# The last four channel tiles of a ConvFFN down projection, moved from plain products to seven block products

## The chip, the cores and the metric

One NeuronCore of a Trainium2 chip runs the whole block for one sequence of 1024 tokens in float32. The metric is device time in microseconds (us) of one execution, and lower is better. Five engines take part: PE (TensorE, matmuls and their weight loads), DVE (VectorE), ACT (ScalarE), POOL (GpSimd) and SP (SyncE, which here only issues transfers). Each runs its own list of instructions in order and waits for the others where it needs their results.

## The reference, cut to what matters

```python
h = rmsnorm(x, norm_mix_g)                      # x: (1, 1024, 1024)
z = h @ w_in                                    # -> A_h, A_B, A_C, B_val, B_gate
yA = A_B * dwconv3(A_C * A_h)
yB = silu(layernorm(dwconv31(B_val * sigmoid(B_gate)) + b))
x = x + concat(yA, yB) @ w_out
h = rmsnorm(x, norm_ffn_g)
g = dwconv3(h @ w_gate)                         # 2816 channels
v = h @ w_up
x = x + (silu(g) * v) @ w_down                  # 2816 -> 1024
return rmsnorm(x, norm_final_g)
```

The change lies in the product with `w_down` and in the final norm, which needs, for every token, the sum of squares over all 1024 outputs.

## The kernel before, in words

Tokens lie along the free axis, in two halves of 512 (`h` = 0 and 1). Channels lie on the 128 partitions: 8 tiles of the model dimension (`d` = 0 to 7) and 22 tiles of the FFN dimension (`f` = 0 to 21). Every float32 operand of a matmul is split into a high and a low part (`split`: ACT copies the high part, DVE subtracts it, L131 and L93), and one product of 128x128 by 128x512 is three matmuls: high by high, high by low, low by high.

**Seven block products.** A product of a 2x2 arrangement of blocks is done with seven block products in place of eight. For the down projection the two rows are two output tiles of a pair `dp` (`m` = 0, 1), the two columns are the token halves, and the inner two are an even and an odd FFN tile. The class `Pair` holds the seven methods. They add into three PSUM banks `a`, `b` and `c`, and after some of them DVE (or ACT and POOL) adds a bank into the residual tile `xf[2*dp+m]`, half `h`:

- `m1` (A11 B11 into `a`) and `m2` (A12 B21 into `b`) both go to (m, h) = (0, 0),
- `m6` (S2 T2 added to `a`) goes to (0, 1), `m7` (S3 T3 added to `a`) to (1, 1), `m4` (A22 T4 added to `a`) to (1, 0),
- `m5` (S1 T1 into `c`) goes to (1, 1), `m3` (S4 B22 added to `c`) to (0, 1).

So the first half of the pair's two tiles is complete with m1, m2, m6, m7 and m4. S1 to S4 are sums of weight blocks, made on POOL (`Sums`, L511) and split on ACT and DVE. T1 to T4 are differences of FFN activations, made on POOL in `ff_done` (L90) when an odd tile `f` is finished; B11, B21, B22 and the T blocks go to DRAM buffers `yd*`, each by a store of 256 KB that SP issues, and come back later through `load_op`, which loads a block and splits it.

**Rounds.** FFN tiles 0 to 17 are worked in NCH = 3 rounds (`ch`) of PPC = 3 pairs of tiles. In a round the four pairs of output tiles come as two couples (`couples`), and the products of a couple stand on PE as m1, then m3 of the couple before, m6, m2, m7, m5, m4. While the last couple of a round runs, `load_op` refills each operand's blocks in the arena `R` as soon as PE has read them.

**The tail.** FFN tiles 18 to 21 (NTAIL = 4) are stored whole in `ytail` and multiplied plainly: `tail_mm` does 4 x 3 matmuls (L152 to L154) for one output tile and one half into a bank `y`. All eight tiles of half 0 come first, then the eight of half 1. After each, `done` adds the bank to the residual on DVE (L1028), ACT squares it (L1030) and DVE adds the square to `accs[h]` (L1032); `scale` multiplies by the norm's weight on ACT (L1024). When half 0 is summed, one matmul with ones (`total3`, L1019) sums over partitions, ACT takes the root (L1067), DVE the reciprocal (L1069, row `rf`), and POOL multiplies the eight tiles of half 0 (`fin`, L1037), which SP stores. For half 1 the last tile is done in three pieces of columns (192, 192, 128): add (L1080), square on DVE (L1081), sum on PE (L1083 to L1085), root, reciprocal (L1092), then `fin` of the eight tiles, five on DVE and three on POOL, and the stores.

**What sets the order.** In blocks under `manual_schedule` the named engines keep the order of the code; the rest, and SP's issues, are ordered by the scheduler when the program is built. In the last block all four computing engines are listed in code order, but they can be filled in among instructions of the block before.

## Time and profile before

| | |
|---|---|
| time, median of 3 runs | 1000.0 us (999.8 to 1000.95) |
| the profiled execution | 1000.93 us, with a span of 999.1 us |
| PE busy | 967.5 us (97%), 4208 matmuls |
| DVE busy | 755.6 us (76%) |
| ACT busy | 452.8 us (45%) |
| POOL busy | 477.0 us (48%) |
| DMA | 112.56 MB, mean 113 GB/s |
| mean granted TensorE clock | 0.993 of full speed |

The span runs from the first to the last instruction of the profiled execution; the time of an execution is 1.8 us more. A row of a timeline gives start, duration, engine, line, operation, out<-in tiles, and in brackets how long the engine sat idle before it and what ended that. A row of the chain of waits gives start, duration and what was done on the path that ended last. Matmuls overlap: one is shown as 0.39 us, but they follow each other at about 0.23 us.

### The profile page before, as it was taken

The numbers are of one execution on the slowest core, as the hardware profiler recorded it, in microseconds if no ns is written. First come the engines' busy times: TensorE is split into PE (matmuls) and PEld (weight loads), VectorE is DVE, ScalarE is ACT, GpSimd is POOL, SyncE is SP. The second block draws the span as 40 slices with busy tenths as digits, with TensorE's granted clock in tenths as the row PEclk, the third lists the DMA queues.
The fourth block names the chain that finished last, engine by engine and source line by source line (L and its number), as shares of the span: only waits on it lengthen the run. The fifth ranks groups of instructions, "written<-read, shape, count | busy, mean of one in ns | idle before, by whom it ended". The sixth has DMA issues, their size and how long they took to land.

```text
span 999.1 us, 11602 instructions
## 1 busy us (share of the span) xinstructions
PE 967.5 (97%) x4208; PEld 790.8 (79%) x4208; DVE 755.6 (76%) x888; ACT 452.8 (45%) x632; POOL 477.0 (48%) x303
## 2 busy tenths in 40 slices
PE   7999999999999999999999999999998999999994
PEld 5788888888878887788888888888886787878883
DVE  7899999999578897855655565565569798796556
ACT  7454422234564456434444443444457263544353
POOL 4289754353853006554455456365336744352006
PEclk9999999999999999999999999999999999999998
DMA  6211111113554204143143133134284663643105
GB/s 257 85 44 63 43 45 61 42 64 106 193 190 153 76 0 158 64 148 106 64 145 108 64 124 129 64 101 141 70 287 130 220 207 96 194 127 109 61 1 169
DMA packets 63274, 112.56 MB, mean 113 GB/s; under 512 B 5488, under 2 KB 27120, under 8 KB 62960
## 3 DMA queue, kind: packets, MB, share of 16 engines
q1 hardware_dynamic: 62640, 110.65, 33.1%
q10 hardware_dynamic: 576, 1.17, 0.3%
q8 instruction: 33, 0.54, 0.2%
q14 instruction: 25, 0.20, 0.1%
HBM read 84.79 MB, written 27.00 MB: 112 GB/s over the span
## 4 chain that ended last, share of the span: by engine, by line
PE 81%; DVE 9%; ACT 3%; issue 2%; DMA 1%; POOL 1%; POOLq 0%; SPq 0%; DVEq 0%; ACTq 0%
PE a L557 30%; PE mm L166 20%; PE c L557 15%; PE b L557 7%; DVE r L93 2%; PE c L692 1%; PE a L692 1%; PE mm L153 1%; PE mm L152 1%; PE mm L154 1%; PE y L154 1%; PE y L152 1%; PE y L153 1%; DMA raw<-wgate 1%; ACT whi L131 1%
## 5 line engine op out<-in xcount | busy, mean ns | idle before, releaser
L166 PE MATMUL mm<-r,whi 128*128 128x512 f32 x576 | 155.8, 389 | 0.0
L557 PE MATMUL a<-r,whi 128*128 128x512 f32 x472 | 145.7, 390 | 0.4 <-ACT a L542 0.4
L323 DVE SCALAR_TENSOR_TENSOR cv<-u,cst,cv 128x512 f32<-128x512 f32 x203 | 138.9, 751 | 1.7 <-ACT cv L317 1.2
L511 POOL TENSOR_TENSOR s<-raw,s 128x512 f32<-128x512 f32 (+1 forms) x31 | 57.5, 1854 | 161.5 <-DVE wlo L93 161.5
L166 PEld LDWEIGHTS mm<-r,whi 128*128 128x128 f32 x576 | 108.1, 188 | 22.6
L557 PE MATMUL c<-r,whi 128*128 128x512 f32 x392 | 121.1, 390 | 0.0
L93 POOL TENSOR_TENSOR wlo<-raw,whi 128x1024 fp32r<-128x1024 f32 x30 | 77.5, 2586 | 88.0 <-ACT whi L131 88.0
L131 ACT ACTIVATE whi<-raw 128x1024 fp32r<-128x1024 f32 (+1 forms) x68 | 69.2, 1020 | 103.5 <-PE mm L166 32.0
L557 PEld LDWEIGHTS a<-r,whi 128*128 128x128 f32 x472 | 88.4, 188 | 19.7 <-ACT a L542 0.8
L511 POOL TENSOR_TENSOR s<-up 128x512 f32<-128x512 f32 (+1 forms) x31 | 42.0, 1354 | 116.7 <-DMA up<-wup 96.8
L557 PE MATMUL a<-r,wlo 128*128 128x512 f32 x236 | 92.2, 391 | 2.8 <-DVE wlo L93 2.8
L166 PE MATMUL mm<-r,wlo 128*128 128x512 f32 x288 | 90.0, 389 | 0.0
L557 PEld LDWEIGHTS c<-r,whi 128*128 128x128 f32 x392 | 73.8, 188 | 16.0
L542 ACT ACTIVATE a<-a 128x512 f32<-128x512 f32 x80 | 47.5, 595 | 66.9 <-PE a L557 64.2
L131 ACT ACTIVATE whi<-s 128x1024 fp32r<-128x1024 f32 (+1 forms) x52 | 52.5, 1010 | 53.5 <-PE c L557 39.8
L557 PE MATMUL c<-r,wlo 128*128 128x512 f32 x196 | 76.5, 390 | 0.0
L635 DVE TENSOR_TENSOR t<-a,c 128x512 f32<-128x512 f32 x40 | 27.5, 687 | 64.4 <-ACT a L542 38.1
L557 PE MATMUL a<-r,ahi 128*128 128x512 f32 x224 | 70.5, 396 | 1.4 <-ACT a L542 1.4
L557 PE MATMUL b<-r,whi 128*128 128x512 f32 x232 | 71.4, 389 | 0.0
L93 DVE TENSOR_TENSOR wlo<-s,whi 128x1024 fp32r<-128x1024 f32 (+1 forms) x52 | 64.2, 1236 | 5.8 <-ACT whi L131 5.7
L131 ACT ACTIVATE r<-r 128x512 fp32r<-128x512 f32 x71 | 43.8, 628 | 49.8 <-DMA r<-ydB 23.3
L166 PEld LDWEIGHTS mm<-r,wlo 128*128 128x128 f32 x288 | 54.1, 188 | 11.2
(214 smaller groups left out, 2142.0 us busy)
## 6 DMA issues: line engine op xcount, KB each, us to landing
raw<-wgate SPq DMA_DIRECT2D x22, 512.0 KB, 4.9
up<-wup SPq DMA_DIRECT2D x20, 512.0 KB, 3.6
raw<-win SPq DMA_DIRECT2D x18, 512.0 KB, 3.2
ydT<-t SPq DMA_DIRECT2D x36, 256.0 KB, 3.4
r<-ydT SPq DMA_DIRECT2D x36, 256.0 KB, 3.3
raw<-wout SPq DMA_DIRECT2D x16, 512.0 KB, 3.4
ydB<-t SPq DMA_DIRECT2D x27, 256.0 KB, 5.0
r<-ydB SPq DMA_DIRECT2D x27, 256.0 KB, 4.5
```

The source lines that it names most:

```text
L93: eng.tensor_tensor(out=out, in0=a, in1=b, op=ALU.subtract)
L131: nc.scalar.activation(hi, y, AF.Copy)
L152: nc.tensor.matmul(out, whi, hi, start=first, stop=False)
L153: nc.tensor.matmul(out, whi, lo, start=False, stop=False)
L154: nc.tensor.matmul(out, wlo, hi, start=False, stop=last)
L166: nc.tensor.matmul(outs[h], w, a[h][z], start=s0, stop=s1)
L323: nc.vector.scalar_tensor_tensor(fin if k == KC - 1 else acc, src, w, acc, ALU.mult, ALU.add)
L511: self.eng.tensor_tensor(out=self.t[:, i * self.w : (i + 1) * self.w], in0=a, in1=b, op=op)
L542: nc.scalar.activation(t, b, AF.Copy)
L557: nc.tensor.matmul(out, w[wz][:, k, :], x[xz], start=first and k + wz + xz == 0, stop=k == n - 1 and wz == 1, skip_group_check=not first)
L635: nc.vector.tensor_tensor(out=out, in0=a, in1=b, op=op)
L692: nc.tensor.matmul(out, w[wz][:, k, :], xz, start=first and k == 0 and wz == 0 and xz is hi, stop=not first and k == 3 and wz == 1)
```

## The change

FFN tiles 18 to 21 become a fourth round (`ch` = 3) with two pairs of tiles (NPL = 2) in place of three. `ytail`, `load_tail`, `tail_prep` and `tail_mm` are gone; `count(ch)` gives the size of a round, and operands, weights and sums take it. The four pairs of output tiles are `fin4`: a4 and b4 are prepared like any couple, c4 and d4 put their split sums into blocks of the arena that are free by then. In the last stretch the code lists the products that complete half 0 (m1, m6, m2, m7, m4) of all four pairs first, then `m5` of a4 and b4, the sum of half 0 (`total3`), m5 of c4 and d4, and m3 of the four; the last of these, `d4`'s, is done in three pieces as before. The additions of squares for three tiles of half 1 go to POOL. The pieces' `fin` are spread as 8, 6 and 5 tiles on DVE in place of 5, 5 and 5. `accs` gets a small pool of its own.

```diff
-NTAIL = NF - 2 * NCH * PPC
+NPL = NF // 2 - NCH * PPC
...
-        if f >= NF - NTAIL:
-            nc.sync.dma_start(ytail[f - (NF - NTAIL)], cc)
-            return
         ys[f] = cc
         if f % 2 == 0:
             return
...
+    def count(ch):
+        return PPC if ch < NCH else NPL
+
+    def xblock(n, o, k, z):
+        return rblocks[OPS.index(o) * 2 * n + z * n + k]
...
     couples = [[Down(ch, 2 * i + e) for e in range(2)] for ch in range(NCH) for i in range(2)]
+    fin4 = [Down(NCH, dp) for dp in range(2)]
+    fin4 += [Down(NCH, 2 + e, rblocks[28 + 2 * e : 30 + 2 * e], rblocks[32 + 2 * e : 34 + 2 * e]) for e in range(2)]
+    couples.append(fin4[:2])
...
-        for i, pair in enumerate(couples):
+        for i, pair in enumerate(couples[:-1]):
             ch = pair[0].ch
-            reload = i % 2 and ch + 1 < NCH
+            reload = i % 2
...
-    def done(b, d, h):
+    def final(d, h, eng=nc.vector, first=0, alone=None):
         x = half(xf[d], h)
-        nc.vector.tensor_tensor(out=x, in0=b, in1=x, op=ALU.add)
-        sq = scr("sq") if d else accs[h]
+        sq = scr("sq") if d != first else accs[h]
         nc.scalar.activation(sq, x, AF.Square)
-        if d and (h, d) != (1, KD - 2):
-            nc.vector.tensor_tensor(out=accs[h], in0=accs[h], in1=sq, op=ALU.add)
+        if d not in (first, alone):
+            eng.tensor_tensor(out=accs[h], in0=accs[h], in1=sq, op=ALU.add)
+        scale(d, h)
         return sq
...
+    a4, b4, c4, d4 = fin4
     with tc.manual_schedule(engines={nc.tensor.engine}):
+        for p in (a4, b4):
+            p.m1()
+        for p in couples[-2]:
+            p.m3()
+        load_op(NCH, "B22")
+        for p in (a4, b4):
+            p.prep3()
+        for p in (a4, b4):
+            p.m6()
+        for p in (c4, d4):
+            p.prep1()
+        for p in (a4, b4):
+            p.m2()
+            final(2 * p.dp, 0)
+        for p in (c4, d4):
+            p.prep2()
+            p.prep3()
+        for p in (a4, b4):
+            p.m7()
+        for p in (c4, d4):
+            p.m1()
+        for p in (a4, b4):
+            p.m4()
+            final(2 * p.dp + 1, 0)
+        for p in (c4, d4):
+            p.m6()
+        for p in (c4, d4):
+            p.m2()
+            final(2 * p.dp, 0)
+        for p in (c4, d4):
+            p.m7()
+        for p in (c4, d4):
+            p.m4()
+            final(2 * p.dp + 1, 0)
+    rf = rup.tile([P, S], F32, tag="up", name="rf")
     with tc.manual_schedule(engines={e.engine for e in (nc.tensor, nc.vector, nc.scalar, nc.gpsimd)}):
...
+        a4.m5()
+        b4.m5()
+        m0 = total3(accs[0])
+        final(1, 1, first=1)
+        std = scr("std")
+        nc.scalar.activation(std, m0, AF.Sqrt, bias=eps_r, scale=1.0 / D)
+        final(3, 1, nc.gpsimd, 1)
+        c4.m5()
+        nc.vector.reciprocal(rf[:, :H], std)
+        d4.m5()
+        final(5, 1, nc.gpsimd, 1)
+        final(7, 1, nc.gpsimd, 1)
+        for dd in range(KD):
+            fin(dd, 0, 0, H, nc.gpsimd)
+            if dd % 2:
+                store(dd // 2, 0, 0, H)
+        a4.m3()
+        final(0, 1, first=1)
+        b4.m3()
+        final(2, 1, first=1)
+        c4.m3()
+        s6 = final(4, 1, first=1, alone=4)
+        d4.mul(d4.c, "S4", "B22", False)
+        last = d4.c
...
-        for (a, b), m in zip(PIECES, ms):
+        for (a, b), m, n in zip(PIECES, ms, (KD, 6, 5)):
...
-                fin(d, 1, a, b, *((nc.vector, rp) if d < 5 else (nc.gpsimd,)))
+                fin(d, 1, a, b, *((nc.vector, rp) if d < n else (nc.gpsimd,)))
```

Three places show how the instructions stand in the two programs.

On PE, before, the sum of half 0 (`total`, L1019) stands among the products of half 1, behind its first two output tiles (the bank `y` ahead of it is tile 1's, the one behind it tile 2's):

```order
L152 MATMUL y_7242<-r3_97,whi_7002 128x512
L153 MATMUL y_7242<-r3_97,whi_7002 128x512
L154 MATMUL y_7242<-r3_97,wlo_7003 128x512
L1019 MATMUL total_7255<-acc_7074,ones_r_91 128x512
L152 MATMUL y_7264<-r3_97,whi_7085 128x512
L153 MATMUL y_7264<-r3_97,whi_7085 128x512
L154 MATMUL y_7264<-r3_97,wlo_7086 128x512
```

On PE, now, with numbers (`a_7256` is d4's bank a, `c_7392`, `c_7401`, `c_7366`, `c_7374` are bank c of c4, d4, a4, b4; `ahi_7224` is A22 of d4, `acc30_7084` the sum of squares of half 0):

```order
L556 MATMUL a_7256<-r0_94,alo_7225 128x512
L986 MATMUL total_7382<-acc30_7084,ones_r_91 128x512
L556 MATMUL c_7392<-r0_94,r1_95 128x512 x6
L556 MATMUL c_7401<-r0_94,r1_95 128x512 x6
L556 MATMUL c_7366<-r1_95,r5_99 128x512 x6
L556 MATMUL c_7374<-r1_95,r5_99 128x512 x6
L556 MATMUL c_7392<-r1_95,r4_98 128x512 x6
L556 MATMUL c_7401<-r1_95,r4_98 128x512 x6
```

The sum moved to directly behind d4's m4, the product that completes half 0; behind it stand m5 of c4 and d4 and the four m3. The m5 of a4 and b4 were filled in earlier, around a4's and b4's m4.

On DVE, before, around the reciprocal of half 0 (`acc_7074` is the tile that holds the sums of squares; all rows here are of half 1):

```order
L1028 TENSOR_TENSOR xd2_5486<-y_7264,xd2_5486 128x512
L1032 TENSOR_TENSOR acc_7074<-acc_7074,sq_7278 128x512
L1069 RECIPROCAL rf_7073<-std_7262 128x512
L1028 TENSOR_TENSOR xd3_5699<-y_7296,xd3_5699 128x512
L1032 TENSOR_TENSOR acc_7074<-acc_7074,sq_7310 128x512
L1028 TENSOR_TENSOR xr0_5700<-y_7314,xr0_5700 128x512
L1032 TENSOR_TENSOR acc_7074<-acc_7074,sq_7328 128x512
L1028 TENSOR_TENSOR xr0_5700<-y_7332,xr0_5700 128x512
L1032 TENSOR_TENSOR acc_7074<-acc_7074,sq_7346 128x512
L1028 TENSOR_TENSOR xr1_5701<-y_7350,xr1_5701 128x512
L1080 TENSOR_TENSOR xr1_5701<-y_7367,xr1_5701 128x192
```

On DVE, now (`acc30` is half 0, `acc31` half 1; `xr0` holds tiles 4 and 5, `xr1` 6 and 7, `xd0` 0 and 1, `xd2` tile 2):

```order
L864 TENSOR_TENSOR xr1_5722<-xr1_5722,a_7256 128x512
L998 TENSOR_TENSOR acc30_7084<-acc30_7084,sq_7347 128x512
L998 TENSOR_TENSOR acc30_7084<-acc30_7084,sq_7358 128x512
L864 TENSOR_TENSOR xr0_5721<-xr0_5721,c_7392 128x512
L1061 RECIPROCAL rf_7363<-std_7386 128x512
L864 TENSOR_TENSOR xr1_5722<-xr1_5722,c_7401 128x512
L864 TENSOR_TENSOR xd0_5497<-xd0_5497,c_7366 128x512
L998 TENSOR_TENSOR acc31_7085<-acc31_7085,sq_7437 128x512
L864 TENSOR_TENSOR xd2_5496<-xd2_5496,c_7374 128x512
L998 TENSOR_TENSOR acc31_7085<-acc31_7085,sq_7448 128x512
L864 TENSOR_TENSOR xr0_5721<-xr0_5721,c_7392 128x512
L1081 TENSOR_TENSOR xr1_5722<-c_7401,xr1_5722 128x192
```

Ahead of the reciprocal now stand the last two additions of half 0 and c4's add; behind it stand two adds, then twice an addition to `acc31` and an add, and then the first piece.

On SP, before, where the FFN's last tiles are stored and the residual tiles 3 to 7 are loaded back (`ytail` is the store of tiles 20 and 21):

```order
L831 DMA raw<-wdown 128x3x128 x2
L831 DMA up<-wdown 128x3x128 x2
L616 DMA ytail<-t 128x1024 x2
L907 DMA xd_5699<-x2d 128x1024
L907 DMA xr_5700<-x2d 128x1024 x2
L907 DMA xr_5701<-x2d 128x1024 x2
```

On SP, now (`ydB` and `ydT` are the operand buffers):

```order
L830 DMA up<-wdown 128x3x128 x2
L623 DMA ydB_1791<-t 128x512
L623 DMA ydT_1795<-t 128x512
L623 DMA ydB_1793<-t 128x512
L623 DMA ydB_1797<-t 128x512
L623 DMA ydT_1792<-t 128x512
L623 DMA ydT_1794<-t 128x512
L623 DMA ydT_1796<-t 128x512
L911 DMA xd_5720<-x2d 128x1024
```

The loads of the residual tiles moved behind seven stores, the last three of which need POOL's differences.

More of the change, by code (lines that the diff above doesn't have):

```diff
@@ L410, in block_kernel @@
     x2d = dpool.tile([KD, P, S], F32, name="x2d")
-    yd = {o: dpool.tile([P, NCH * PPC, H], F32, name=f"yd{o}") for o in OPS}
-    ytail = dpool.tile([NTAIL, P, S], F32, name="ytail")
+    yd = {o: dpool.tile([P, NF // 2, H], F32, name=f"yd{o}") for o in OPS}
     def out_done(pt, dt, h, acc):
@@ L855, in prep3 @@
+            self.w.update(self.s.first(self.raw, self.up, self.h12))
         def prep3(self):
[L856 to L857 removed]
+            self.w.update(self.s.second(self.raw, self.up, a22p, self.h34))
         def out(self, m, h):
@@ L970, in block_kernel @@
                     load_op(ch + 1, o)
-    free = rblocks[:16]
-    def yblock(h, i, z):
-        return free[h * 8 + 2 * i + z]
-    def load_tail(h):
-        for i in range(NTAIL):
-            load_split(yblock(h, i, 0), yblock(h, i, 1), ytail[i, :, h * H : h * H + H])
-    tw = {}
-    def tail_prep(dp):
-        hl = hilo()
-        for e in range(2):
-            d = 2 * dp + e
-            raw = wraw.tile([P, NTAIL * P], F32, tag="raw", name="rawt")
-            nc.sync.dma_start(raw.rearrange("p (f m) -> p f m", m=P), wdown[d, :, NF - NTAIL :])
-            a = e * NTAIL * P
-            sl = [t[:, a : a + NTAIL * P] for t in hl]
-            split(raw, *sl, nc.vector)
-            tw[d] = parts(sl, 0, NTAIL)
-    def tail_mm(b, d, h):
-        for i in range(NTAIL):
-            mm3(b, tw[d][0][:, i, :], tw[d][1][:, i, :], yblock(h, i, 0), yblock(h, i, 1), i == 0, i == NTAIL - 1)
-    load_tail(0)
-    tail_prep(0)
-    b0 = []
-    with tc.manual_schedule(engines={nc.tensor.engine}):
-        for d in range(2):
-            b0.append(bank("y"))
-            tail_mm(b0[d], d, 0)
-        for p in couples[-1]:
-            p.m3()
-    load_tail(1)
-    rf = rup.tile([P, S], F32, tag="up", name="rf")
+    tq = open_pool("tq", 1)
+    accs = [tq.tile([P, H], F32, name=f"acc3{h}") for h in range(2)]
+    rf = None
     def scr(name):
         return cpy.tile([P, H], F32, tag="c", name=name)
-    acc3 = wsum.tile([P, S], F32, tag="s", name="acc")
-    accs = [half(acc3, h) for h in range(2)]
     def total3(a):
```

68 lines of the change are left out of this document (20 added, 48 removed).

## The prediction

> **What bounds the kernel now.** I read the page's first part, then the windows of the last 100 us, the chain of waits there, and last the timelines of single engines.
>
> ```profile
> PE 967.5 (97%) x4208; PEld 790.8 (79%) x4208; DVE 755.6 (76%) x888; ACT 452.8 (45%) x632; POOL 477.0 (48%) x303
> ```
>
> ```profile
> 900.00:934.00 34.00, 34.00 (x150) 27.97 (x149) 23.52 (x34) 12.98 (x21) 6.89 (x6) 1.00 0.40 123
> 934.00:968.00 34.00, 34.00 (x149) 27.78 (x148) 15.70 (x23) 15.36 (x23) 0.00 (x0) 1.00 0.00 2
> ...
> 974.20:982.70 8.50, 8.50 (x39) 6.82 (x37) 6.41 (x9) 4.07 (x6) 8.30 (x6) 1.00 0.33 124
> 982.70:986.10 3.40, 2.57 (x15) 2.12 (x14) 3.30 (x8) 1.77 (x3) 3.28 (x3) 1.00 0.41 154
> 986.10:999.10 13.00, 0.49 (x2) 0.30 (x2) 7.34 (x19) 2.23 (x6) 4.64 (x9) 0.70 0.64 202
> ```
>
> The columns are PE, weight loads, DVE, ACT, POOL, clock, DMA share and GB/s. PE is busy all the time up to 982; DVE is half empty before 968 and then loaded; after 986 PE has nothing left. The chain of waits tells where the one bound gives way to the other:
>
> ```profile
> 929.76 4.20 PE a L557 x18
> ...
> 939.43 4.08 PE c L557 x18
> ...
> 965.28 0.86 PE total L1019 x2
> ...
> 968.65 0.24 PE y L154
> 968.89 0.02 issue
> 968.91 0.70 DVE xd L1028
> ```
>
> Up to 968.89 the path is nothing but PE. From there it stays on DVE and ACT, though PE works on: the vector side and PE run neck and neck to the end of the products. A matmul costs 4.08 / 18 = 0.227 us. The stretch that the change rewrites begins where the last m4 of the third round ends, at 929.76 + 4.20 = 933.96.
>
> The vector side behind it, DVE first, then ACT, then POOL:
>
> ```profile
> 970.91 3.35 DVE L1069 RECIPROCAL rf<-std 128x512 f32<-128x512 f32 x1
> 974.17 0.63 DVE L1028 TENSOR_TENSOR xd<-y,xd 128x512 f32<-128x512 f32 x1
> 975.50 0.75 DVE L1032 TENSOR_TENSOR acc<-acc,sq 128x512 f32<-128x512 f32 x1 [0.70 <-ACT sq L1030]
> 976.17 0.68 DVE L1028 TENSOR_TENSOR xr<-y,xr 128x512 f32<-128x512 f32 x1
> 977.55 1.66 DVE L1032 TENSOR_TENSOR acc<-acc,sq 128x512 f32<-128x512 f32 x1 [0.70 <-ACT sq L1030]
> 979.13 0.68 DVE L1028 TENSOR_TENSOR xr<-y,xr 128x512 f32<-128x512 f32 x1
> 980.50 1.65 DVE L1032 TENSOR_TENSOR acc<-acc,sq 128x512 f32<-128x512 f32 x1 [0.70 <-ACT sq L1030]
> 982.08 0.68 DVE L1028 TENSOR_TENSOR xr<-y,xr 128x512 f32<-128x512 f32 x1
> 982.68 0.34 DVE L1080 TENSOR_TENSOR xr<-y,xr 128x192 f32<-128x192 f32 x1
> ```
>
> ```profile
> 967.45 1.28 ACT L1067 ACT_TABLE_LOAD   x1
> 968.75 0.69 ACT L1067 ACTIVATE std<-total,eps_r 128x512 f32<-128x512 f32 x1
> 969.64 0.63 ACT L1030 ACTIVATE sq<-xd 128x512 f32<-128x512 f32 x1 [0.20 <-DVE xd L1028]
> 970.30 0.73 ACT L1024 ACTIVATE xd<-xd,cst 128x512 f32<-128x512 f32 x1
> ```
>
> ```profile
> 974.40 1.29 POOL L1037 TENSOR_TENSOR xd<-xd,rf 128x512 f32<-128x512 f32 x1 [63.03 <-DVE rf L1069]
> ```
>
> The steps to keep: from an add to its square 0.73 (968.91 to 969.64), from a square to the next thing that uses it 0.66 (969.64 to 970.30), a scaling 0.73, the addition of a square 0.69 alone but 1.65 while POOL multiplies. Two of three additions paid the latter.
>
> **The products.** Removed: 8 tiles x 2 halves x 12 = 192 matmuls. Added: 4 pairs x 7 products x 6 = 168. Unhindered, PE ends 24 x 0.227 = 5.4 us earlier. That reaches the end only if the vector side follows.
>
> **When half 0 is complete.** Behind 933.96 PE now does 18 matmuls of the third round's last m3, 5 products x 4 pairs x 6 = 120, and the 12 of a4's and b4's m5 that were filled in: 150 x 0.227 = 34.0, so d4's m4 ends at 967.96. Before it took 18 + 96 = 114 matmuls, to 959.8. All the products of half 0 now stand ahead, so half 0 ends 8 us later.
>
> **The new wait.** `total` stands directly behind on PE. Until it may run: d4's add starts on DVE at 967.98. ACT is still busy with c4's tile, whose m4 ended 6 matmuls earlier, at 966.60: square at 967.35, scaling from 968.01 to 968.74. So d4's square starts at 968.74, its addition at 969.40 and ends at 970.09. PE waits 970.09 - 967.96 = 2.1 us, and behind the waiting instruction are queued m5 of c4 and d4 and all four m3. `total` takes 0.86, to 970.95; c4's m5 six matmuls, to 972.31; its add on DVE starts at 972.33, and the reciprocal 0.60 later (982.08 to 982.68), at 972.93. ACT is no gate: scaling to 970.13, table 1.30 (967.45 to 968.75), root 0.69, done at 972.12. The reciprocal starts 972.93 - 970.91 = 2.0 us later than before.
>
> **Behind the reciprocal.** It holds DVE 3.26 us (970.91 to 974.17), to 976.19. Then d4's c at 976.19; its square at 976.92; POOL adds it at 977.58, for 1.29 (the row of a POOL operation of this size), to 978.87, and goes on with the multiplications of half 0. DVE adds a4's c at 976.80; ACT's scaling holds the square until 978.31, the addition comes at 978.97, just after POOL has begun: 1.65, with the next add 1.58 after its start (977.55 to 979.13), at 980.55. Square 981.28, addition 981.94, 1.65 again, c4's add at 983.52, first piece at 984.12. Before it was 982.68: 1.4 us later. PE's last product is done by 970.95 + 36 x 0.227 = 979.1 and delays nothing. If both additions took 0.69 instead, it would be 1.9 less.
>
> ```profile
> 987.79 1.15 DVE L1037 TENSOR_TENSOR xd<-xd,rp 128x192 f32<-128x192 f32 x4 [0.40 <-ACT rf L1093]
> 988.86 0.35 DVE L1037 TENSOR_TENSOR xr<-xr,rp 128x192 f32<-128x192 f32 x1
> 989.12 1.35 DVE L1092 RECIPROCAL rp<-std 128x192 f32<-128x192 f32 x1
> ```
>
> **The pieces.** Five multiplications take 989.12 - 987.79 = 1.33 us, 0.27 each. The first piece has three more and the second one more on DVE, ahead of the next reciprocal: 4 x 0.27 = 1.1 us. POOL, which did them before, is still at half 0 by then (from 978.87, eight of at least 1.29).
>
> **What I cost at nothing.** The fourth round needs 14 block splits for 8, and 16 weight splits where `tail_prep` had 8: 14 more on DVE, and 8 more bank adds.
>
> ```profile
> L93 DVE TENSOR_TENSOR wlo<-rawt,whi 128x512 fp32r<-128x512 f32 x8 | 5.4, 690 | 3.4 <-ACT whi L131 3.4
> ```
>
> At 0.69 that is 22 x 0.69 = 15.2 us; DVE is idle for 10.5 + 18.3 us in the two windows from 900 to 968, and so covers it, ACT the same (12.98 and 15.36 busy), POOL's 16 sums find it empty, and the 1.5 MB more of operand loads meet a DMA share of 0.40 and 0.00. Without that cover, each late split would stop PE.
>
> **The early part.**
>
> ```profile
> 774.36 9.84 SPq L616 DMA_DIRECT2D ytail<-t  x2
> 784.30 0.38 SPq L907 DMA_DIRECT2D xd<-x2d  x1
> ```
>
> ```profile
> L90 POOL TENSOR_TENSOR t<-t 128x512 f32<-128x512 f32 x36 | 54.8, 1533 | 15.3 <-DVE t L614 15.3
> ```
>
> ```profile
> 789.37 0.69 DVE L863 TENSOR_TENSOR xd<-xd,a 128x512 f32<-128x512 f32 x1 [1.91 <-DMA xd<-x2d]
> ...
> 801.30 2.52 DVE L93 TENSOR_TENSOR r<-r 128x512 fp32r<-128x512 f32 x2 [2.29 <-ACT r L131]
> ```
>
> ```profile
> 810.00:820.00 10.00, 10.00 (x45) 8.17 (x44) 10.00 (x14) 6.49 (x11) 4.49 (x4) 1.00 0.42 131
> ```
>
> ```profile
> 834.52 4.35 PE L557 MATMUL a<-r,r 128*128 128x512 f32 x18 [1.41 <-DVE xd L863]
> ```
>
> SP loads the residual tiles as soon as tile 21 is stored. Now three of POOL's differences, 1.53 each, must come first: some 4.2 us later after the issue of stores in between. DVE's add at 789.37 waits for such a load, and in order behind it stands all that follows. DVE's idle 2.29 us before 801.30 covers over half; smaller gaps cover most of the rest. What is left delays a stretch in which DVE is full, and where PE waited 1.41 us for it in the end. I take 0.3 us; the ends are 0 and 4.2 - 2.29 = 1.9.
>
> **The sum.** 1.4 + 1.1 + 0.3 = 2.8 us: a span of 1001.9 and, for the profiled execution of 1000.93, 1003.7. That execution lies 0.9 above the median, so for the median 1000.0 + 2.8 = **1002.8 us**. About 0.2%, or 2.0 us, is what a measurement of this kernel can tell from no change.
>
> **A clock that may fall.** PE's wait of 2.1 us could cost more than itself:
>
> ```profile
> 776.33 3.35 PE L557 MATMUL a<-r,r 128*128 128x512 f32 x7 [2.76 <-DVE r L93]
> ```
>
> After a wait of 2.76 us seven matmuls took 3.35 us, half speed; after the 1.41 us above, 18 took 4.35, nearly full speed. At half speed c4's m5 takes 1.36 longer and the reciprocal follows. 2.1 lies between the two; the 2.76 came behind other short waits, so I take no loss, with 1.36 as the other end. The Trainium skill (TensorE: Matmul & The Clock Gate, section "Why this matters for your kernels") warns only of gaps over about 3 us, one idle window. By that rule this gap costs nothing and the sum stays 2.8; by the row of 2.76 us, which shows the loss below that limit, it would be 4.2.
>
> **Rivals.** (1) *The hand-over to the down projection gets shorter, and the time is not slower.*
>
> ```profile
> 747.06 0.69 DVE L93 TENSOR_TENSOR r<-r,r 128x512 fp32r<-128x512 f32 x1 [5.38 <-ACT r L131]
> ```
>
> The build moves two bank adds of the FFN into this idle gap, which were behind it. If DVE's queue to 776.33 thereby runs 1.2 us earlier (two of 0.60), PE's wait of 2.76 falls to 1.6 and the half-speed stretch, 3.35 - 7 x 0.227 = 1.8, goes: 3.0 less, no early cost, -0.5, 999.5. It decides at whether DVE works without a gap from 747 to 776:
>
> ```profile
> 757.51 0.63 ACT L131 ACTIVATE r<-r 128x512 fp32r<-128x512 f32 x1 [1.38 <-DMA r<-ydB]
> ```
>
> Against it: at 757.51 the queue still waits for a load, which the adds do not bring forward. Chance 0.25.
>
> (2) *Loads and clock both cost.* 2.8 + 1.36 + 1.6 = 5.8, 1005.8. For it speak the rows of 776.33 and 789.37. Chance 0.15.
>
> (3) *The shorter products set the end:* -5.4 + 1.1 + 0.3 = -4.0, 996.0. It decides at whether the reciprocal starts before about 966, so that DVE meets the last product. Against it: half 0 is complete only at 967.96. For it only that DVE is half empty before. Chance 0.08.
>
> **How the numbers follow.** The forecast has 0.52, of which 0.12 with one addition or none blocked, so within 0.2%. Rival 1 gives 0.18 within and 0.07 faster (with both additions unblocked it reaches -2.4). Slower: 0.40 + 0.15 = 0.55; within: 0.30; faster: 0.07 + 0.08 = 0.15. The range reaches down to no blocked addition and no wait at `total`, 2.8 - 1.9 - 2.1 = -1.2, 998.8, and up to rival 2, 1005.8; it leaves out rival 3 and parts of 1 and 2, some 0.2. The likeliest case alone spans 1000.9 to 1004.2.
>
> **What would show it.** Right: in the changed profile PE waits some 2 us at `total` for DVE, the reciprocal of half 0 starts 5 us after d4's m4, additions behind it take about 1.65, and PE ends its products some 5 us before the first piece. Wrong: `total` without a wait, the first piece right behind d4's m3, or the last m4 of the third round ending more than 1 us away from 933.96.

## The result: slower by 0.95%, and the profile after

The changed kernel takes 1009.51 us (median of 4 runs, 1008.04 to 1011.07) where the kernel before took 999.9 beside it: a ratio of 1.0095, with a 95% interval from 1.0077 to 1.0112. The profiled execution took 1009.25 us, with a span of 1007.3, 8.2 us more than before. Slower was forecast, and for the reasons that were given at the end of the program; but the size, 9.6 us against a forecast 2.8, lies outside the range. Most of the rest came from a step that the forecast had put at 0.3 us.

The page's first part of the changed kernel:

```profile
PE 968.9 (96%) x4184; PEld 791.6 (79%) x4184; DVE 774.5 (77%) x911; ACT 461.2 (46%) x650; POOL 510.6 (51%) x330
```

There are 24 fewer matmuls (4184 for 4208), as the change says, and yet PE's busy time went up: some of them ran slowly. The chain of waits says where the time was lost, if one looks for the last m4 of the third round (18 of the 30 matmuls in the first row; the other 12 are a4's and b4's m1) and for the last 18 matmuls ahead of the sum of half 0:

```profile
935.26 6.95 PE a L556 x30
...
968.16 4.13 PE a L556 x18
972.29 0.02 issue
972.32 0.70 DVE xr L864
...
975.85 1.12 PE total L986 x2
...
979.00 3.35 DVE rf L1061
```

That m4 started at 929.76 before and starts at 935.26 now: **5.5 of the 8.2 us are lost before the rewritten stretch begins.** From there to the first piece (990.19 below) it is 54.93 us for 52.92 (982.68 before), 2.0 more, and from there to the end of the span 17.1 for 16.4, 0.7 more.

**Where the 5.5 us went.** The issue of transfers by SP, from the last stores of FFN tiles 20 and 21 to the loads of the residual tiles:

```profile
786.16 0.80 SPq L623 DMA_DIRECT2D ydB<-t  x2
789.00 3.84 SPq L623 DMA_DIRECT2D ydT<-t  x3
793.01 0.32 SPq L911 DMA_DIRECT2D xd<-x2d  x1
793.50 1.78 SPq L911 DMA_DIRECT2D xr<-x2d  x4
```

The load of tile 3, which was issued at 784.30, now comes at 793.01, 8.7 us later: the three `ydT` stores ahead of it are drawn out to 792.84, each waiting for a difference. POOL's timeline tells why, and DVE's what followed (the brackets: idle before, and what ended it):

```profile
783.04 2.01 POOL L90 TENSOR_TENSOR xd<-xd,a 128x512 f32<-128x512 f32 x1
785.01 2.00 POOL L510 TENSOR_TENSOR s<-s,raw 128x384 f32<-128x384 f32 x1
786.96 5.54 POOL L90 TENSOR_TENSOR t<-t 128x512 f32<-128x512 f32 x3
...
797.26 1.27 POOL L90 TENSOR_TENSOR xd<-xd,a 128x512 f32<-128x512 f32 x1 [0.58 <-DMA xd<-x2d]
```

```profile
797.22 0.69 DVE L864 TENSOR_TENSOR xd<-xd,a 128x512 f32<-128x512 f32 x1 [4.31 <-DMA xd<-x2d]
798.56 1.28 DVE L864 TENSOR_TENSOR xd<-xd,c 128x512 f32<-128x512 f32 x2 [0.65 <-POOL xd L90]
```

The 8.7 us are three delays in a row. DVE's last product for tile 21 ended at 786.13 in place of 783.84, which is 2.3 us; POOL then still had a sum of weights in hand and began the differences at 786.96, 0.8 us on; and it needed 1.85 us for each of the three, 5.5 in all, where the forecast had 1.53. DVE's rows for that product, before and now:

```profile
781.52 2.32 DVE L614 TENSOR_TENSOR t<-t 128x1024 f32<-128x1024 f32 x1
```

```profile
783.82 2.31 DVE L613 TENSOR_TENSOR t<-t 128x1024 f32<-128x1024 f32 x1
```

When the load is late, DVE stands still for 4.31 us at tile 3's add. PE's rows follow. The first is the hand-over to the down projection: the same wait of 2.76 us as before, ended 2.0 us later (776.33 before), but without the half clock that followed it there (seven matmuls in 1.89 us for 3.35). So the first m4 starts only 0.4 us late. The second row and the windows behind it show that PE pays twice for the late load (a window's last three columns are the granted clock, the DMA share and GB/s):

```profile
778.32 1.89 PE L556 MATMUL a<-r,r 128*128 128x512 f32 x7 [2.76 <-DVE r L93]
...
799.30 2.07 PE L556 MATMUL c<-r,r 128*128 128x512 f32 x4 [4.67 <-DVE xd L864]
```

```profile
799.30:801.40 2.10, 2.10 (x5) 1.72 (x6) 1.41 (x2) 0.00 (x0) 0.84 (x2) 0.50 1.02 405
801.40:803.50 2.10, 2.10 (x6) 1.61 (x6) 0.00 (x0) 0.30 (x1) 0.98 (x1) 0.50 1.10 345
```

A wait of 4.67 us, and then a granted clock of 0.50 in both windows. From the first m4 of the down projection to the next couple's are 35.98 us for 28.71 before: 7.3 more, of which 2.6 are left for the clock. Against this stand later waits that the kernel before had and this one has not (1.41 us at 834.52 among them); DVE has caught up by then.

**The end** went nearly as worked out. DVE, then PE and POOL:

```profile
973.71 0.69 DVE L864 TENSOR_TENSOR xr<-xr,a 128x512 f32<-128x512 f32 x1 [0.71 <-PE a L556]
974.32 1.48 DVE L998 TENSOR_TENSOR acc<-acc,sq 128x512 f32<-128x512 f32 x2
978.39 0.69 DVE L864 TENSOR_TENSOR xr<-xr,c 128x512 f32<-128x512 f32 x1 [2.60 <-PE c L556]
979.00 3.35 DVE L1061 RECIPROCAL rf<-std 128x512 f32<-128x512 f32 x1
...
985.04 1.73 DVE L998 TENSOR_TENSOR acc<-acc,sq 128x512 f32<-128x512 f32 x1 [1.55 <-POOL acc L998]
...
988.13 1.55 DVE L998 TENSOR_TENSOR acc<-acc,sq 128x512 f32<-128x512 f32 x1 [0.76 <-ACT sq L996]
...
990.19 0.35 DVE L1081 TENSOR_TENSOR xr<-c,xr 128x192 f32<-128x192 f32 x1
```

```profile
975.85 1.12 PE L986 MATMUL total<-acc,ones_r 128*128 128x512 f32 x2 [2.18 <-DVE acc L998]
976.41 8.77 PE L556 MATMUL c<-r,r 128*128 128x512 f32 x36
```

```profile
983.70 1.30 POOL L998 TENSOR_TENSOR acc<-acc,sq 128x512 f32<-128x512 f32 x1 [2.51 <-ACT sq L996]
984.96 5.84 POOL L1004 TENSOR_TENSOR xd<-xd,rf 128x512 f32<-128x512 f32 x4
```

PE's new wait is there (2.18 us), the reciprocal follows c4's add, both additions of squares on DVE are stretched by POOL's multiplications, and PE ends its products at 985.2, 5 us before the first piece.

### The profile page after: what moved, and what is told of

Same layout as the page of the kernel before. It is cut to its first block, busy times and chain, and to the rows that moved or that the text cites. A ratio compares the mean times of both kernels' runs of the same rounds, so it can differ in the third digit from the quotient of the medians.

```text
span 1007.3 us, 11712 instructions
## 1 busy us (share of the span) xinstructions
PE 968.9 (96%) x4184; PEld 791.6 (79%) x4184; DVE 774.5 (77%) x911; ACT 461.2 (46%) x650; POOL 510.6 (51%) x330
## 3 DMA queue, kind: packets, MB, share of 16 engines
q10 hardware_dynamic: 576, 1.17, 0.3%
## 4 chain that ended last, share of the span: by engine, by line
PE 78%; DVE 10%; DMA 4%; ACT 3%; issue 3%; POOL 2%; ACTq 0%; SPq 0%; POOLq 0%; DVEq 0%
PE a L556 30%; PE mm L166 19%; PE c L556 15%; PE b L556 7%; DVE r L93 2%; PE mm L274 2%; PE c L688 1%; PE a L688 1%; DMA raw<-wout 1%; DVE wlo L93 1%; DMA raw<-wgate 1%; DMA r<-ydB 1%; ACT whi L131 1%; DVE r L214 1%; DVE t L610 1%
## 5 line engine op out<-in xcount | busy, mean ns | idle before, releaser
L556 PE MATMUL a<-r,whi 128*128 128x512 f32 x496 | 154.8, 393 | 0.3 <-ACT a L541 0.3
L510 POOL TENSOR_TENSOR s<-raw,s 128x512 f32<-128x512 f32 (+2 forms) x35 | 60.5, 1729 | 170.9 <-DVE wlo L93 160.4
L131 ACT ACTIVATE whi<-raw 128x1024 fp32r<-128x1024 f32 (+2 forms) x72 | 71.7, 998 | 107.7 <-PE b L556 33.3
L556 PEld LDWEIGHTS a<-r,whi 128*128 128x128 f32 x496 | 94.1, 190 | 21.0 <-ACT a L541 0.7
L510 POOL TENSOR_TENSOR s<-up 128x512 f32<-128x512 f32 (+2 forms) x35 | 46.0, 1315 | 117.3 <-DMA up<-wup 96.5
L556 PE MATMUL a<-r,wlo 128*128 128x512 f32 x248 | 97.5, 393 | 2.9 <-DVE wlo L93 2.9
L90 POOL TENSOR_TENSOR t<-t 128x512 f32<-128x512 f32 x44 | 69.0, 1579 | 20.0 <-DVE t L613 20.0
L131 ACT ACTIVATE whi<-s 128x1024 fp32r<-128x1024 f32 (+2 forms) x54 | 53.7, 995 | 52.2 <-PE c L556 42.3
L556 PE MATMUL a<-r,ahi 128*128 128x512 f32 x240 | 75.7, 396 | 1.2 <-ACT a L541 1.2
L93 DVE TENSOR_TENSOR wlo<-s,whi 128x1024 fp32r<-128x1024 f32 (+2 forms) x54 | 66.7, 1236 | 5.9 <-ACT whi L131 5.7
```

Source lines behind the costliest of these rows:

```text
L90: nc.gpsimd.tensor_tensor(out=out, in0=a, in1=b, op=op)
L93: eng.tensor_tensor(out=out, in0=a, in1=b, op=ALU.subtract)
L131: nc.scalar.activation(hi, y, AF.Copy)
L510: self.eng.tensor_tensor(out=self.t[:, i * self.w : (i + 1) * self.w], in0=a, in1=b, op=op)
L556: nc.tensor.matmul(out, w[wz][:, k, :], x[xz], start=first and k + wz + xz == 0, stop=k == n - 1 and wz == 1, skip_group_check=not first)
```

## The experiments

Two questions: what makes the start late, and what makes the end late. Times are medians beside runs of the kernel before on the same chip (1000.4 to 1001.0); the 95% interval of the ratio to it is in brackets. "The stretch" is from the start of the first m4 of the down projection to the start of the last m4 of its third round: 783.69 to 929.60 before, 145.9 us; 784.12 to 935.10 now, 151.0 (starts by the timeline, which lie 0.16 us ahead of the chain's). Four kernels below change only the end of the program (after_total, after_m5, tail_pe, tail_pe_total); in them the stretch takes 150.2 to 151.4 us, while PE's wait near 798 goes from 2.56 to 4.96. So single profiles can be compared by the stretch to about 1 us, and hardly by that one wait.

### The start

**before_t**: the kernel before, with the differences and the T stores added for the tail's tiles.

```diff
...
             nc.sync.dma_start(ytail[f - (NF - NTAIL)], cc)
-            return
...
+            if f < NF - NTAIL or o[0] == "T":
                 nc.sync.dma_start(yd[o][:, f // 2, :], half(t, h))
```

> The kernel before, with POOL's differences for tiles 19 and 21 and four T stores for each added; nothing reads them. Theory Q (the 5.4 us by which the last m4 of the third round is late come from the loads of the residual tiles, held behind stores and buffers that wait for POOL's differences): the first load of tile 3 moves from 784.3 to about 792, PE then waits over 3 us for DVE near 798, that m4 ends near 939, and the time is 1004 to 1006 us. Rival H (they come from the fourth round's own loads, splits and weights, or from the way the build fills them in): the m4 stays within 1 us of 934.0 and the time is at most 1001.5 us.

1005.17 us, 1.0048 [1.0033, 1.0063]: theory Q. The first load of tile 3 and PE's wait, in its trace:

```profile
791.91 0.32 SPq L907 DMA_DIRECT2D xd<-x2d  x1
```

```profile
797.92 2.08 PE L557 MATMUL c<-r,r 128*128 128x512 f32 x4 [4.40 <-DVE xd L863]
```

The stretch takes 150.7 us. Nothing else of the change is in this kernel, and it loses 4.7 us: half of the whole loss.

**before_t19** has the same for tile 19 alone (`if f % 2 == 0 or f == NF - 1: return`).

> The kernel before with POOL's differences and the four T stores for tile 19 alone (nothing reads them). Theory L (tile 21's differences, ahead of the loads of the residual tiles, cost nearly all of the 4.7 us that both cost): within 1 us of the kernel before, at most 1001.5 us. Rival K (tile 19's, which delay the first loads of operands at the hand-over, cost as much): 1002.5 us or more.

1002.29 us, 1.0020 [1.0010, 1.0029], between the two theories: some 1.9 us are tile 19's and, by subtraction, 2.8 tile 21's. The stretch is as short as before (785.44 to 930.98, 145.5), and it starts 1.75 us late, so in this profile what tile 19's differences cost lies ahead of it. So there were two early costs, and the prediction had looked at one. The split is not firm: in before_t's profile the stretch alone is 4.8 us longer, and in the changed kernel and its variants, which all have tile 19's differences, it starts anywhere from 781.94 to 785.77.

**after_nodiff** leaves tile 21's last three differences out (`if f < NF - 1:` ahead of them, the stores from `yo`).

> The changed kernel without the three differences of tile 21 that need its last half (T2, T3 and T4 are stored from tile 21 itself, so that part of the result is left out); the seven stores stay. Theory Q: the first load of tile 3 is issued near 789 in place of 793.0, PE's wait of 4.7 us falls under 2 us and the half clock behind it goes, the last m4 of the third round ends at 934 to 936.5 and the time is 1004 to 1006.5 us. Rival H: that m4 stays near 939 and the time at 1008 to 1010 us.

1008.70 us, 1.0084 [1.0067, 1.0101], above theory Q's range and in rival H's, though the stretch fell to 148.2 us and PE's wait from 4.67 to 2.42. The load was issued at 790.28, not 789: SP had another wait ahead of it, loads of weights that wait for POOL's sums.

**after_dve** puts T2 and T4 of tile 21 on DVE.

> The changed kernel with two of those three differences (T2 and T4) on DVE, which needs about 0.6 us for one, in place of POOL; nothing is left out. Theory Q: the differences are done near 789 in place of 792.5, the load is issued near 790, and the time is 1005 to 1008 us. Rival D (DVE is so full there that 1.3 us more of work on it costs what the load gains): 1008.5 to 1011 us.

1007.26 us, 1.0066 [1.0048, 1.0083]: theory Q's range. The load came at 788.99; PE's waits were 1.17 us at 796.67 and 2.20 at 838.09; the stretch took 148.1.

**slot_b** and **slot_act** ask whether SP's order holds the load or the place in memory. slot_b lets tile 3 take a place that no late block held; slot_act also issues its load by ACT.

```diff
-    xd3 = xrp.tile([P, S], F32, name="xd3")
-    xdr = [xrp.tile([P, 2, S], F32, name=f"xr{i}") for i in range(2)]
+    x1 = xrp.tile([P, 2, S], F32, name="xr1")
+    xd3 = xrp.tile([P, S], F32, name="xd3")
+    x0 = xrp.tile([P, 2, S], F32, name="xr0")
+    xdr = [x0, x1]
...
-        for d in range(3, KD):
+        with urgent():
+            nc.scalar.dma_start(xd3, x2d[3])
+        for d in range(4, KD):
             load_xd(d)
```

> The changed kernel with the residual tiles placed the other way round in their pool, so that tile 3 takes a place in memory that is free long before, while SP's order stays. Theory O (the order on SP holds the load: it stands behind stores that wait for POOL): the load of tile 3 is still issued near 793, and the time is 1008 to 1010.5 us. Rival M (its place in memory holds it): the load is issued under 790 and the time is 1005 to 1007.5 us.

1009.23 us, 1.0088 [1.0073, 1.0103]; the load at 791.87, behind stores that end there: SP's order, not memory.

> As slot_b, and the load of tile 3 is issued by ACT in place of SP, past the stores. Theory O: it is issued near 788.5, DVE no longer waits 4.3 us for it, PE's wait of 4.7 us falls under 2 us, the last m4 of the third round ends 2.5 to 4.5 us earlier than in the changed kernel (at 935 to 937), and the time is 1005 to 1007 us. Rival H (something else makes that part late): the m4 stays at 939 and the time at 1008.5 us or more.

1010.36 us, 1.0101 [1.0086, 1.0116]. The load got past the queue, at 784.93, and nothing was won: theory O fell. The trace shows who took its place (ACT's queue, DVE, PE):

```profile
784.93 0.34 ACTq L955 DMA_DIRECT2D xd<-x2d  x1
```

```profile
790.65 0.68 DVE L864 TENSOR_TENSOR xd<-xd,a 128x512 f32<-128x512 f32 x1
797.22 1.28 DVE L864 TENSOR_TENSOR xd<-xd,c 128x512 f32<-128x512 f32 x2 [5.89 <-POOL xd L90]
```

```profile
797.97 2.08 PE L556 MATMUL c<-r,r 128*128 128x512 f32 x4 [5.51 <-DVE xd L864]
```

DVE's add to tile 3 no longer waits, but the next one waits for POOL's own add to the same tile, which stands on POOL behind the three differences, four sums of weights and one more add. Two chains of equal length hold DVE, both begun by POOL's differences.

**both_nodiff** takes both away.

> Both ways at once: tile 21's last three differences left out (T2, T3 and T4 are stored from tile 21 itself, so that part of the result is left out) and the load of tile 3 issued by ACT. Theory W (two chains of about equal length hold DVE: the load of tile 3 behind SP's stores, and POOL's own add to tile 3 behind the differences; with one of them gone the other still binds): DVE's wait near 795 goes, PE waits under 1.5 us there, the last m4 of the third round ends at 934 to 936, and the time is 1003.5 to 1005.5 us. Rival H (the fourth round's other loads make that part late): the m4 stays at 937 or later, 1006.5 us or more.

1008.40 us, 1.0071 [1.0056, 1.0086], above theory W's range and in rival H's; the last m4 starts at 933.40 and so ends past 937, which was rival H's sign too. PE's wait near 797 is gone and the stretch is 147.6 us, so the two chains were what held it there; but short waits came at 815.72, 829.16 and 838.63 (1.08, 0.79, 0.99 us), the stretch started 2.1 us late, the clock fell behind the sum of half 0 (last section), and the time hardly moved.

**early_dve** (all three differences on DVE, the load by ACT, nothing left out) and **early_add** (also tile 3's early add on DVE):

```diff
-                self.add_copy(m, h, copy_of(self.a, "a1"))
+                t = copy_of(self.a, "a1")
+                if m and self.e:
+                    self.add(m, h, t)
+                else:
+                    self.add_copy(m, h, t)
```

> The changed kernel with all three of tile 21's last differences on DVE and the load of tile 3 issued by ACT; nothing is left out. Theory W: both chains are shorter, DVE has 1.8 us more to do; the m4 ends at 935 to 937.5 and the time is 1004.5 to 1007 us. Rival D (DVE is so full up to 835 that its extra work comes back as a later wait of PE): the m4 at 938 or later, 1007.5 us or more.

1007.17 us, 1.0066 [1.0049, 1.0082]; the stretch 148.7, PE's wait 2.43 at 797.20. Just above theory W's range, just under rival D's.

> early_dve with one more edit: the first add to the second half of tile 3 is made by DVE in place of POOL. Theory P (what still held DVE for 3.7 us was POOL's add, behind POOL's four sums of weights): DVE's wait near 795 goes, PE waits under 1 us there in place of 2.4, the first to the last m4 of the down projection take at most 147 us in place of 148.7, and the time is 1005 to 1006.5 us. Rival D (DVE's queue is full, and the wait comes back later): 148 us or more, and 1007 us or more.

1007.91 us, 1.0071 [1.0058, 1.0084]: rival D. The stretch takes 148.6 us; the wait near 797 is gone, and a new one stands 39 us on:

```profile
836.35 5.96 PE L556 MATMUL a<-r,r 128*128 128x512 f32 x18 [2.15 <-DVE xd L864]
```

These 18 matmuls took 5.96 us, where the kernel before needs 4.35 behind its 1.41 us: the clock fell here. best2 (below) has the same start and a wait of 2.02 us in this place, kept its clock, and needs 147.0 us for the stretch. So 1.6 of the 148.6 are the clock's.

**free_all** was to show that this is DVE being full: early_add's edits with the three differences left out.

> early_add with tile 21's last three differences left out on every engine (T2, T3 and T4 are stored from tile 21 itself, so that part of the result is left out): DVE has 1.9 us less to do than in early_add. Theory D (DVE is the bound from 780 to 836, and whatever is put on it comes back as a wait of PE there): PE's wait near 836 falls to at most 1.2 us, near the 1.41 us of the kernel before, the first to the last m4 of the down projection take at most 146.8 us (148.6 in early_add, 145.9 in the kernel before), and the time is 1003.5 to 1006 us. Rival N (other work of the fourth round makes that part late): 148 us or more, 1007 us or more.

1009.38 us, 1.0085 [1.0068, 1.0102]. Theory D fell, and the numbers are rival N's: with 1.9 us less on DVE, PE's wait is 2.39 us at 838.21, the clock falls behind it as in early_add, and the stretch is 151.0. In this trace the first blocks of the next round were split later (DVE waited 3.60 us for them before 803.14; 2.29 before 801.30 in the kernel before). Whether that or something else of the fourth round holds PE near 838 stays open.

Put together: added to the kernel before, the differences and their stores are enough to lose 4.7 us, with the same wait in the same place. Left out of the changed kernel, tile 21's last three give back 0 to 3.4 of the stretch's 5.1 us (after_nodiff, both_nodiff, free_all) and 0.1 to 1.1 us of time. So they are a cause that was shown, but they are not shown to be the only one; other work of the fourth round (rivals H and N) is not excluded.

### The end

**after_total** puts the sum of half 0 behind m5 of c4 and d4 on PE (m5 of a4 and b4 are written where the build had filled them in).

```diff
+        c4.m5()
+        d4.m5()
...
         m0 = total3(accs[0])
...
-        c4.m5()
         nc.vector.reciprocal(rf[:, :H], std)
-        d4.m5()
```

> The changed kernel with the sum of half 0 on PE behind m5 of c4 and d4 in place of ahead of them, so that PE has 12 matmuls (2.7 us) to do while it would wait 2.2 us. Theory V (the vector side sets the end): PE's wait goes, the reciprocal starts within 0.7 us of where it did, one add of 0.6 us moves ahead of it, the first piece comes 0 to 1 us earlier, and the time is 1008.5 to 1009.5 us. Rival P (PE's wait is what delays the end): the whole 2.2 us come back, 1007.0 to 1007.5 us.

1007.56 us, 1.0073 [1.0058, 1.0088]: some 2 us below the changed kernel: below theory V's range and just above rival P's, but not by rival P's way. In its trace the reciprocal and the first piece:

```profile
978.44 3.35 DVE L1062 RECIPROCAL rf<-std 128x512 f32<-128x512 f32 x1 [1.18 <-ACT std L1060]
...
988.23 0.34 DVE L1081 TENSOR_TENSOR xr<-c,xr 128x192 f32<-128x192 f32 x1
```

The reciprocal is 0.56 us earlier, as theory V had it, and from it to the first piece are 9.79 us for 11.19: one add fewer behind it, and a shorter wait for POOL's addition.

**after_m5** puts m5 of a4 and b4 behind the sum of half 0 as well, which completes half 0 12 matmuls sooner.

> The changed kernel with m5 of c4 and d4, then the sum of half 0, then m5 of a4 and b4 behind d4's m4 (in the changed kernel m5 of a4 and b4 was filled in ahead of it): half 0 is complete 12 matmuls (2.7 us) earlier and PE does not wait. Theory V: the reciprocal starts 2 to 2.7 us earlier, but two adds and their squares that were done before now stand behind it (some 1.3 us each), so the first piece comes 0 to 2 us earlier and the time is 1007.5 to 1009.5 us. Rival R (when half 0 is complete is what sets the end): 2.7 us or more come back, at most 1006.8 us.

1007.59 us, 1.0073 [1.0051, 1.0095]: theory V. The reciprocal started at 976.06, 2.9 us earlier, and the first piece at 988.37, no earlier than in after_total. When half 0 is complete does not set the end; what DVE does behind the reciprocal does.

**tail_pe** sums the squares of tiles 0 and 2 of half 1 on PE, for each piece.

```diff
-            nc.tensor.matmul(m[:, a:b], ones, s6[:, a:b], start=False, stop=False)
+            for t in (s0, s2, s6):
+                nc.tensor.matmul(m[:, a:b], ones, t[:, a:b], start=False, stop=False)
```

> The changed kernel with the squares of tiles 0 and 2 of half 1 summed by PE (two more matmuls with ones for each piece) in place of added by DVE; that takes the two additions out of DVE that meet POOL's multiplications. Theory V (DVE sets the end: two additions of 1.6 to 1.7 us and the waits ahead of them): the first piece starts at 985 to 986.5 in place of 990.2, and since ACT's squares and PE's sums stand behind it, the time is 1004.5 to 1006.5 us. Rival S (PE's sums, two more of some 0.5 us for each piece, and ACT's squares take the place): 1008 to 1010 us.

1006.44 us, 1.0056 [1.0040, 1.0071]: theory V. The two stretched additions are gone, and the first piece (986.56) follows four adds in a row. The kernel before pays for two such additions as well (1.66 and 1.65 us, in the prediction's rows), so what comes back here is not something that the change had lost. In the profiled execution part of the gain was lost again: PE's wait at the sum was the same as before the edit, 2.17 us, but the clock fell behind it.

```profile
976.25 10.28 PE L556 MATMUL c<-r,r 128*128 128x512 f32 x36
```

```profile
976.20:978.60 2.40, 2.40 (x6) 1.59 (x5) 0.00 (x0) 1.96 (x4) 0.04 (x1) 0.50 0.00 0
```

36 matmuls took 10.28 us where the changed kernel's took 8.77, and the reciprocal started at 980.36 in place of 979.00, though the sum had begun 0.25 us earlier (975.60 for 975.85): 1.6 us of loss. The prediction had named this possibility and priced six of the matmuls behind the sum, at 1.36 us; the sum itself ran slowly as well.

**tail_pe_total** has both edits of the end.

> The changed kernel with the sum of half 0 behind m5 of c4 and d4, and the squares of tiles 0 and 2 of half 1 summed by PE: both edits of the end together. Theory V (the vector side sets the end, and PE's wait of 2.2 us costs again when the clock halves behind it): PE has no wait of over 1 us between 960 and 980, the reciprocal starts near 978.4, the first piece at 983 to 984.5, and the time is 1002 to 1004.5 us. Rival F (POOL's eight multiplications of half 0, which end near 994, then hold the last pieces): 1005 us or more.

1003.82 us, 1.0026 [1.0015, 1.0037]: theory V. No wait at the sum, no fall of the clock, and DVE's rows are

```profile
978.06 3.35 DVE L1062 RECIPROCAL rf<-std 128x512 f32<-128x512 f32 x1 [1.18 <-ACT std L1060]
981.33 1.22 DVE L864 TENSOR_TENSOR xd<-xd,c 128x512 f32<-128x512 f32 x2
982.47 0.68 DVE L864 TENSOR_TENSOR xr<-xr,c 128x512 f32<-128x512 f32 x1
983.06 0.35 DVE L1081 TENSOR_TENSOR xr<-c,xr 128x192 f32<-128x192 f32 x1
```

5.00 us from the reciprocal to the first piece, for 11.19. The two edits give back 5.7 us of the 9.6 by the medians, 6.9 by the ratios, without touching the start. That is more than the 2.7 us that the end had lost, since the stretched additions are a cost of the kernel before too.

**best** joins this with early_dve, and **best2** adds early_add and puts ACT's scalings of tiles 0, 2 and 4 behind the first piece's root.

> early_dve and both edits of the end in one kernel. If the parts add, 1009.5 less 3.5 (early) less 6 (end): 998 to 1001.5 us, about the kernel before. If the early gain is taken back by waits of PE later on: 1002 us or more.

1001.50 us, 1.0010 [1.0000, 1.0019]: in the range, at its upper end.

> best with early_add's edit, and with ACT's scalings of tiles 0, 2 and 4 of half 1 behind the root of the first piece in place of between their squares. Theory A (the first root waits for ACT's squares, which stand behind scalings): it comes 1 to 1.5 us sooner after the first piece (2 us in place of 3.2), and the time is 998 to 1000 us, below the kernel before. Rival F (POOL's multiplications of half 0, to near 991.8, set the end): 1000.5 us or more.

1000.20 us, 1.0000 [0.9989, 1.0011]: the same as the kernel before, just above theory A's range. The first root came 1.87 us after the first piece (978.65 and 980.52), as expected. What the chain of waits follows at the end now is POOL:

```profile
974.21 1.31 POOL acc L1006
...
978.26 5.21 POOL xd L1013 x4
983.47 5.98 POOL xr L1013 x6
```

None of the versions beat the kernel before beyond the interval. The kernel before was not tried with its own stretched additions taken away, so no run here compares the two kinds of product at an equally short end.

## Why the prediction was right or wrong

The prediction's own sign of being wrong came: the last m4 of the third round ends near 939.4, far from 933.96. Its signs of being right, all of them at the end, came too.

- **The products, half 0, the new wait: right.** Counted from the last m4 of the third round, d4's add came 0.2 us after its forecast, PE's wait was 2.18 us for 2.1, PE's products ended 0.6 late. The reciprocal came 0.57 us late (0.26 at the start of the sum, 0.26 in the sum, which took 1.12 us, not 0.86, and 0.04 in c4's m5), and everything behind it carried those 0.57 on: first piece 2.0 us later than before, for 1.4.
- **The blocked additions: right**, 1.73 and 1.55 us for 1.65. The first of them waited for POOL's own addition to the same tile, not for ACT's scaling as forecast; the two ended within 0.2 us of each other, which is luck. The Trainium skill (SBUF — State Buffer, section "Who interferes with whom") says that a DVE operation with two inputs in SBUF and a GpSimd operation that reads SBUF lock each other out, and the first to issue keeps the ports; the trace agrees (0.69 us alone, 1.55 to 1.73 beside POOL), and taking the two additions away was worth 3.1 us by the medians (tail_pe).
- **The pieces: 0.7 us for 1.1.** Up to POOL's last multiplication the 1.1 is right: by the chains it starts 12.4 us after the first piece, 11.3 before (994.00 and 1002.56). What follows it was 0.4 us shorter. So the end as a whole, 2.7 us for a forecast 2.5, is closer than its parts, 0.6 over and 0.4 under; that closeness is luck.
- **What was costed at nothing: right for the fourth round itself.** From 939.4, where the third round's last m4 ends, to 973.7, where d4's m4 ends, PE is busy for 34.27 of 34.30 us. Whether the fourth round's work costs something further ahead is part of what the experiments left open.
- **The early part: the step that failed.** It said "some 4.2 us later", "DVE's idle 2.29 us before 801.30 covers over half", "I take 0.3 us; the ends are 0 and 1.9". The load came 8.7 us later, DVE stood still for 4.31, PE for 4.67, and then ran at half clock for over 4 us; the stretch lost 5.1. before_t shows 4.7 us for the differences of tiles 19 and 21 and their stores alone. Three things were wrong in it. Only POOL's three differences were counted, and they at 1.53 us in place of 1.85 (three times 1.53 are 4.6, not 4.2; it is not said where the 0.4 go); tile 21 itself came 2.3 us later, POOL was not free at once, and its differences held its own add to tile 3 as well (slot_act). DVE's idle time ahead was taken off the delay, though it lies behind PE's wait, not ahead of it. And tile 19's differences, ahead of the hand-over to the down projection, were not costed at all (1.9 us, before_t19). The upper end of the range was built on the same slack, so the range missed too.
- **The rivals.** A shorter hand-over (1): it did not come; the first m4 is 0.4 us later, in a profile without the half clock that the kernel before had there. That half clock was worth 1.6 us (5.80 us from the end of the wait to the first m4, for 7.36), so the hand-over itself came 2.0 us later. Loads and clock (2) was the nearest: the loads cost more than its 1.9, and the clock fell at 799 instead of at the sum. Shorter products (3): no; but best2's end shows that the vector side can be made to follow them.
- **Not settled.** The trace has 8.2 us, 5.5 of them ahead of the rewritten stretch, but the medians lie 9.6 apart, and part of the 5.5 is not traced to a single cause (above). The changed kernel's median lies 4.3 us above before_t's; between their two profiles 4.4 us lie, 3.0 of them at the end, 1.1 ahead of the first m4 (784.12 for 783.00) and 0.3 in the stretch. The 1.1 is within what the start of that m4 varies among the variants.

## What to carry to other kernels

Price a moved store by the engine that makes its data and by what that engine has queued at that moment, and follow the engine's own later work too: here the same three operations held a load and an add on two queues, and freeing one showed only the other. Idle time of an engine covers a delay only if it lies between the delay and the point where the next engine starts to wait. And fewer products were worth nothing here while the work behind the last sum (DVE's additions beside a multiplying POOL) could not follow: PE ended its products 5 us before the first piece. With that work shortened (best2) the time is that of the kernel before, not less.

## What the runs showed of the hardware

The same idle gap of PE costs different amounts. Behind a wait of 2.76 us the granted clock was 0.50 for 3.1 us in the kernel before, and 1.00 in the changed kernel:

```profile
776.30:779.40 3.10, 3.07 (x7) 2.49 (x8) 3.10 (x3) 1.06 (x1) 3.02 (x3) 0.50 0.06 22
```

```profile
778.30:781.40 3.10, 3.08 (x13) 2.55 (x14) 3.10 (x3) 1.09 (x2) 3.10 (x3) 1.00 0.00 0
```

So it was behind 2.17 and 2.18 us at the sum: 0.50 in tail_pe (its window stands above), and 1.00 in the changed kernel:

```profile
976.00:978.40 2.40, 2.40 (x9) 1.65 (x10) 0.01 (x1) 2.36 (x4) 0.00 (x0) 1.00 0.00 0
```

How often this happens can be counted over the profiles. At the hand-over 17 of them have a wait of 2.72 to 2.76 us. In 14 the time from its end to the first m4 is 7.4 us, in three (after, slot_act, tail_pe_total) 5.8: a loss of 1.6 us, or none. At the sum ten have a wait of 2.17 or 2.18 us. From the last m4 of the third round to the reciprocal seven of them take 43.9 us, and three 44.7 (slot_act), 45.5 (both_nodiff) and 45.5 (tail_pe). The shortest wait with a fall behind it was early_add's 2.15 us; behind 2.20 us in after_dve there was none.

The prediction weighed a rule of the Trainium skill (TensorE: Matmul & The Clock Gate, section "Why this matters for your kernels") by which only gaps over about 3 us count; these rows show a halved clock after gaps of 2.17 and 2.76 us, and the measurement decides. The same page (section "Part 1: The HAM clock gate") says that activity is watched in a window that runs freely, so that the moment at which the clock changes depends on where the window stands; that would fit the differing outcomes, though no run here shows the window itself. In this kernel a gap of some 2.2 to 2.8 us on PE is best priced with both ends: itself, and itself with up to 1.6 us of half speed behind it. And two single profiles differ by up to 1.6 us for each such gap, whatever the kernels do.
